# One group of eight PSUM banks for every accumulator, in a two-layer hybrid encoder

## The chip, the cores and the metric

The kernel runs on one core of one Trainium2 chip. The metric is device time in microseconds (us) of one execution, launch to end, on that core; lower is better. The profile splits the core into TensorE (PE: matmuls and transposes; PEld its weight loads), VectorE (DVE), ScalarE (ACT), GpSimd (POOL), SyncE (SP, which here only issues transfers) and the DMA engines. PE writes its results to PSUM, which has eight banks of 512 float32 per partition; a tile of this kernel's PSUM pool is one whole bank. DVE and ACT read the results from there.

## The reference, cut to what matters

Two layers, 512 tokens, width 1024, all in float32. Each layer is a feed-forward block, a mixer with three kinds of attention, and a second feed-forward block:

```
for l in range(2):
    h = h + 0.5 * rmsnorm(swiglu(rmsnorm(h), w_gu, w_down))         # FFN 1, inner width 2816
    u = rmsnorm(h); proj = u @ w_in[l]                              # q,k,v of A, B, C and the gates
    oa = neighbourhood_attention(qa, ka, va, rpb)                   # 8 heads, bias table, window on a grid
    ob = sliding_window_attention(rope(qb), rope(kb), vb, sink)     # 8 heads, |i-j| <= 128, a sink logit
    oc = differential_attention(rope(qc), rope(kc), vc, lam)        # 4 heads x 2 maps, dense 512 x 512
    merged = sum_i sigmoid(gate_i) * (o_i @ w_branch_i)
    h = h + rmsnorm(merged @ w_out)
    h = h + 0.5 * rmsnorm(swiglu(rmsnorm(h), w_gu2, w_down2))       # FFN 2
```

## The kernel before, in words

Every float32 operand is split into a high part (rounded by ACT) and a low part (the rest, by DVE), and each product of 128 x 128 blocks is three matmuls, L298, L299 and L300 in `mm3`. `dense1` (L317) makes one 128 x 512 block of a projection this way: 8 blocks deep, so 24 matmuls into one bank (12 for a branch product). The weights stream in tiles of 512 KB; ACT and DVE split them half a tile at a time (L199, L200), which serves 12 matmuls, and four such halves may wait ahead.

`bank(tag)` (L144) hands out a PSUM tile. There are three tags: `mm` with four banks (projections, FFN products), `at` with three (attention scores, transposes, small sums) and `o` with one (attention outputs and sums).

The feed-forward blocks are matmuls of the same kind (L842, L1082) with little else in between; a good part of them and the handovers stand in a region in which PE, ACT and DVE keep the order of the program text.

The mixer (L1387 on) is a list of units, `ORDER` (L68), written in this order: `qa`, `kb`, `qb`, `qc` make queries, keys and values; `aa`, `ab`, `ac` are the attention of branch A and B (one unit is two heads) and of C (one unit is one head with its two maps); `g..` are gates and `y..` the products with `w_branch`, 24 of each. Around the three kinds of attention the list reads `qa0 qa1 aa0 aa1 qa3 qa2 aa3 aa2 kb ga2 ga1 ...`, `... ab0 qb1 ...  ab1 ... ab3 ab2 ...` and `... ac0 yb0 yb1 qc2 ... ac1 ... ac2 ... ac3`. A scheduler makes from it one fixed order of instructions for each engine: it prefers what is written first and takes something written later when the first is not ready by its own reckoning or has no buffer. On the chip each engine takes its list strictly in order, except that waits are by semaphore.

One head of A or B is `softmax_pv` (L1329):

- four blocks of 128 queries: two matmuls of scores each (L1337, L1338) into an `at` bank; DVE adds the bias and takes the row extreme (L1341); ACT does the exponential and the row sum (L1350). B has two small steps for its sink (L1347 on DVE ahead of the exponentials, L1353/L1354 behind them);
- one reciprocal (L1355) and four scalings (L1357) on DVE;
- for four blocks of keys: PE transposes (L1365) into an `at` bank, ACT makes the high part (L324), DVE the low part (L325), PE multiplies both with the values into the `o` bank (L1368, L1369);
- ACT and DVE add the two halves of the `o` bank up (L1371, L1372).

The scores are ten blocks of 128 x 128 a head (2, 3, 3 and 2), so are the transposes. One head of C is `attn_c` (L1464): 16 score matmuls of 512 columns (L1475, L1476), eight row maxima (L1477) and exponentials (L1482), reciprocals, scalings and differences on DVE (L1486 to L1490), 16 transposes (L1498), 12 value matmuls (L1501 to L1503), and then a copy, a square and a row sum (L1505, L1508, L1511).

In a layer there are thus 8 heads of A, 8 of B and 4 of C.

Of the kernel before, what the change touches and what calls it, by code (L numbers as in the profile page):

```python
# [10 lines left out]
F32 = mybir.dt.float32  # L11
# [5 lines left out]
P = 128  # L17
# [3 lines left out]
T = 512  # L21
# [9 lines left out]
WARM = 9  # L31
PAD = {"f": 184, "m": 184}
SECOND = 1
KS = 8
KP = KF - 2 * KS
HOLD_OUT = ("g", "g", "g", "g", "g", "tx", "tx", "pt")
# [73 lines left out]
def encoder_kernel(ctx: ExitStack, tc: tile.TileContext, order, xT, wts, cols, rows, rpb, consts, tables, out):  # L110
# [5 lines left out]
    ps = ctx.enter_context(tc.tile_pool(name="ps", bufs=1, space=PSUM))  # L116
# [2 lines left out]

    BUFS = {"X": 6, "n": 2, "wr": 3, "wp": 4}  # L120
    ABUFS = {"f": {"t": 4, "x": 10}, "m": {"t": 5, "h": 4, "rr": 2, "tx": 5, "st": 16, "g": 10, "s": 2, "pt": 4}}
    PBUFS = {"mm": 4, "at": 3, "o": 1}

    def open_phase(kind):
        pool = ExitStack()
# [5 lines left out]
    def nm(s):  # L131
        serial[0] += 1
        return f"{s}{serial[0]}"

    def big(tag, dt=F32, shape=(P, T), name="v"):
        if tag in BUFS:
            return sb.tile(list(shape), dt, tag=tag, name=nm(name), bufs=BUFS[tag])
        kind, pool = phase[0]
        return pool.tile(list(shape), dt, tag=tag, name=nm(name), bufs=ABUFS[kind][tag])
# [2 lines left out]
        return sb.tile([P, w], F32, tag=tag, name=nm(tag), bufs=bufs)  # L142

    def bank(tag):  # L144
        return ps.tile([P, T], F32, tag=tag, name=nm(tag), bufs=PBUFS[tag])

    V, A, G, PE = nc.vector, nc.scalar, nc.gpsimd, nc.tensor

# [83 lines left out]
    def quarter(k, u):  # L232

        return KP + KS * (int(k[1]) - 1) + 2 * u, HB * (int(k[0]) - 1)

    for l in range(L):
        for which in (1, 2):
            name = f"ffn{which}_w_down"
            places = {(k, u): quarter(k, u) for k in ("11", "12", "21", "22") for u in range(KS // 2)}
            places.update({(f"n{n + 1}", u): (2 * u, HB * n) for n in range(2) for u in range(KP // 2)})  # L240
# [5 lines left out]
    def sum_up(l, which):  # L246
# [3 lines left out]
        def begin_sum(key, u):  # L250
            t = dr.tile([P, 2, T], F32, tag="sum", name=nm("sum"), bufs=L * 2 * 2 * (KS // 2))
            G.dma_start(t, down[l, which, ("21", u)])
            sums[l, which, (key, u)] = t

        def add_to(key, more, u):
            G.dma_start(sums[l, which, (key, u)], down[l, which, (more, u)], accum_op=ALU.add, max_dma_last_dim=4096)

        for key, more in (("s3", "11"), ("s1", "22")):
            steps.extend((lambda key=key, u=u: begin_sum(key, u)) for u in range(KS // 2))
            steps.extend((lambda key=key, more=more, u=u: add_to(key, more, u)) for u in range(KS // 2))  # L260
        return steps
# [14 lines left out]
    def first_loads(hT):  # L276
        def load(hs, *bs):
            for b in bs:
                nc.sync.dma_start(hT[:, b, hs], xT[b * P : (b + 1) * P, hs])

        load(HALVES[0], 0)
        fetch(2, nc.sync)
        load(HALVES[0], 1, 2)
        fetch(1, nc.sync)
        load(HALVES[0], 3, 4, 5)
        fetch(1, nc.sync)
        load(HALVES[0], 6, 7)
        load(HALVES[1], *range(KD))
        nc.sync.dma_start(cons, consts)
        warm = bank("o")  # L290
        for _ in range(WARM):
            PE.matmul(warm[:, :P], ones, ones, start=True, stop=True)
        V.tensor_scalar(out=half, in0=colt, scalar1=0.5, scalar2=None, op0=ALU.mult)
# [8 lines left out]
    def dense(blocks, X, tags=("mm",), i=None, accs=None, ws=None, midway=None, hooks={}):  # L302
        accs = accs or [bank(tags[n % len(tags)]) for n in range(len(blocks))]
        kept = []
        for k in range(len(X)):
            if midway and k == len(X) // 2:
                midway()
            x = X[k] if i is None else (X[k][0][:, i, :], X[k][1][:, i, :])
            for n, (acc, (name, l, r0, c)) in enumerate(zip(accs, blocks)):
                w = ws[k * len(blocks) + n] if ws else wblk(name, l, r0 + k, c)  # L310
                kept.append(w)
                mm3(acc if i is None else acc[:, HALVES[i]], w, x, k == 0, k == len(X) - 1)
            if k in hooks:
                hooks[k]()
        return (accs, kept) if i == 0 else accs

    def dense1(name, l, c, X, r0=0, tag="mm", midway=None):  # L317
        return dense([(name, l, r0, c)], X, (tag,), midway=midway)[0]
# [13 lines left out]
    def spread(r, nt):  # L332
        rep = bank("at")
        for t in range(nt):
            PE.matmul(
                rep[:, t * P : (t + 1) * P], r[:, t : t + 1].to_broadcast([P, P]), ident, start=True, stop=True
            )
        return rep[:, : nt * P]
# [1048 lines left out]
    def mixer(l, op, first):  # L1387
        w, X = "w_in", op.blocks
        second = [dense1(w, l, c + 1, X) for c in (QA, KA)[:SECOND]]
        cosR = big("rr", name="cosR")  # L1390
# [280 lines left out]
def build(order):  # L1671
    import concourse.bacc as bacc

    nc = bacc.Bacc("TRN2", target_bir_lowering=False, num_devices=1)
    shapes = {
        "xT": (D, T),
        "wts": (NTILES, P, WB * P),
        "cols": (P, NCOLS),
        "rows": (L * ROWW,),
        "rpb": (L * 8 * 16 * RPBW,),  # L1680
        "consts": (P, CONSTW),
        "tables": (P, TABLEW),
    }
    args = [nc.dram_tensor(f"in_{n}_dram", s, F32, kind="ExternalInput").ap() for n, s in shapes.items()]
    args.append(nc.dram_tensor("out_0_dram", (D, T), F32, kind="ExternalOutput").ap())
    with tile.TileContext(nc) as tc:
        encoder_kernel(tc, order, *args)
    return nc
# [35 lines left out]
```

## Time and profile before

| | before |
|---|---|
| time, median of 3 runs | 2442.7 us (2439.57 to 2444.72) |
| the profiled execution's own time | 2441.57 us |
| its span, first to last instruction | 2439.8 us |
| matmuls on PE | 14298 |
| busy share of PE, DVE, ACT | 99%, 74%, 55% |
| stretch from 390 to 790 us (mixer, layer 0) | 400 us, of them DVE busy 279.26 us, ACT 225.40 us |
| stretch from 1610 to 2010 us (mixer, layer 1) | 400 us, of them DVE busy 280.95 us, ACT 224.40 us |

The profile is one execution, taken by the hardware; its time is 1.1 us under the median of the runs. In its rows a group or a timeline entry names the line of the kernel, the engine, the operation, and the tiles written and read (`at<-cons,s`: writes an `at` bank, reads the constants and the scores `s`). A timeline row begins with its start in us and its length in us; in square brackets stands how long the engine was idle before and what released it. Matmuls are pipelined: the step from one start to the next is what a matmul costs, not its listed length. A windows row gives a stretch, its length, and the busy time of each engine with its number of instructions, then the clock that TensorE was granted (1.00 is full speed), the share of the DMA engines and GB/s.

### The profile page before, as it was taken

What the parts mean: (1) busy time and instruction counts of PE and PEld (TensorE: products, weight loads), DVE (VectorE), ACT (ScalarE), POOL (GpSimd) and SP (SyncE); (2) the same over time, 40 slices, a digit from 0 to 9 for tenths busy, and PEclk for the clock granted to TensorE, in tenths of its full rate; (3) what the DMA queues carried; (4) which work ended last, traced back from release to release, by engine and by line L of the source; (5) the groups of instructions that cost most, each with busy time, mean ns of one, the idle gap of its engine ahead of it and who ended that gap; (6) DMA issues with size and microseconds to landing.
All of it is one profiled execution on the core that took longest, in us unless ns stands there. A gap on an engine that the chain in (4) does not pass through costs nothing. (4 is left out here: it accounts for less than half of the span.)

```text
span 2439.8 us, 37786 instructions
## 1 busy us (share of the span) xinstructions
PE 2404.1 (99%) x14298; PEld 2111.5 (87%) x14298; DVE 1797.8 (74%) x2943; ACT 1347.5 (55%) x2471; POOL 192.1 (8%) x192
## 2 busy tenths in 40 slices
PE   9999999999999999999999999999999999999998
PEld 8999888888877889998899998888877778899987
DVE  8887976857667467888878878776676764788786
ACT  6555655646555365555655555555465554555553
POOL 0111000000111100110001110000001111011100
PEclk9999999999999999999999999999999999999999
DMA  5566536445442334654435565373454333356642
GB/s 170 162 163 182 169 132 175 116 113 149 111 131 95 111 105 132 169 154 162 170 95 157 156 173 190 116 183 106 113 143 124 110 103 121 96 147 165 184 144 87
DMA packets 119190, 340.59 MB, mean 140 GB/s; under 512 B 15968, under 2 KB 22752, under 8 KB 118496
## 3 DMA queue, kind: packets, MB, share of 16 engines
q1 hardware_dynamic: 91344, 224.85, 29.9%
q10 hardware_dynamic: 22032, 79.78, 10.9%
q0 software_dynamic: 5632, 33.56, 6.8%
q8 instruction: 112, 1.84, 0.3%
q14 instruction: 70, 0.57, 0.1%
HBM read 285.16 MB, written 48.23 MB: 137 GB/s over the span
## 5 line engine op out<-in xcount | busy, mean ns | idle before, releaser
L298 PE MATMUL mm<-X,w 128*128 128x512 f32 (+1 forms) x1044 | 397.1, 380 | 2.2 <-ACT w L199 1.7
L299 PE MATMUL mm<-X,w 128*128 128x512 f32 (+1 forms) x1044 | 396.8, 380 | 0.7 <-DVE X L522 0.7
L300 PE MATMUL mm<-X,w 128*128 128x512 f32 (+1 forms) x1044 | 396.1, 380 | 0.0
L200 DVE TENSOR_TENSOR w<-wr,w 128x512 fp32r<-128x512 f32 x360 | 255.3, 714 | 168.2 <-ACT w L199 167.0
L199 ACT ACTIVATE w<-wr 128x512 fp32r<-128x512 f32 x360 | 223.4, 627 | 226.6 <-PE mm L300 184.3
L842 PE MATMUL mm<-ht,l 128*128 128x256 f32 x1120 | 316.5, 283 | 0.0
L842 PE MATMUL mm<-ht,h 128*128 128x256 f32 x1120 | 316.3, 282 | 0.0
L842 PE MATMUL mm<-lt,h 128*128 128x256 f32 x1120 | 315.6, 282 | 0.0
L298 PEld LDWEIGHTS mm<-X,w 128*128 128x128 f32 x1044 | 197.4, 189 | 34.0 <-ACT w L199 1.9
L299 PEld LDWEIGHTS mm<-X,w 128*128 128x128 f32 x1044 | 197.2, 189 | 32.2 <-DVE X L522 1.1
L300 PEld LDWEIGHTS mm<-X,w 128*128 128x128 f32 x1044 | 197.1, 189 | 31.4
L842 PEld LDWEIGHTS mm<-ht,l 128*128 128x128 f32 x1120 | 213.1, 190 | 0.0
L842 PEld LDWEIGHTS mm<-ht,h 128*128 128x128 f32 x1120 | 213.0, 190 | 0.0
L842 PEld LDWEIGHTS mm<-lt,h 128*128 128x128 f32 x1120 | 212.7, 190 | 0.0
L1082 PE MATMUL mm<-wh,f 128*128 128x512 f32 x640 | 200.3, 391 | 0.0
L842 PE MATMUL mm<-X,h 128*128 128x256 f32 x1120 | 200.3, 279 | 0.0
L842 PEld LDWEIGHTS mm<-X,h 128*128 128x128 f32 x1120 | 171.2, 189 | 0.3
L842 PE MATMUL mm<-X,l 128*128 128x256 f32 x560 | 155.4, 278 | 0.0
L1082 PEld LDWEIGHTS mm<-wh,f 128*128 128x128 f32 x640 | 120.3, 188 | 26.9
L702 DVE TENSOR_TENSOR l<-wr,h 128x1024 fp32r<-128x1024 f32 x70 | 85.7, 1224 | 78.5 <-PE mm L842 78.5
L1082 PE MATMUL mm<-wl,f 128*128 128x512 f32 x320 | 126.6, 396 | 3.1 <-DVE wl L959 3.1
L324 ACT ACTIVATE hi<-at 128x256 fp32r<-128x256 f32 (+2 forms) x168 | 77.2, 474 | 73.4 <-PE at L1365 37.9
(366 smaller groups left out, 5458.5 us busy)
## 6 DMA issues: line engine op xcount, KB each, us to landing
wr<-in_wts_dram SPq DMA_DIRECT2D x223, 512.0 KB, 4.7
wr<-in_wts_dram ACTq DMA_DIRECT2D x152, 512.0 KB, 3.6
sum<-in_wts_dram POOLq DMA_DIRECT2D x64, 512.0 KB, 5.5
st<-hi SPq DMA_DIRECT2D x84, 128.0 KB, 2.5
st<-lo SPq DMA_DIRECT2D x84, 128.0 KB, 3.4
ap<-in_wts_dram SPq DMA_DIRECT2D x20, 512.0 KB, 6.7
a<-kept SPq DMA_DIRECT2D x32, 256.0 KB, 5.9
ap<-sum SPq DMA_DIRECT2D x16, 512.0 KB, 4.7
```

The costliest lines, as they stand in the source:

```text
L199: A.activation(hi, raw, AF.Copy)
L200: V.tensor_tensor(out=lo, in0=raw, in1=f(hi), op=ALU.subtract)
L298: PE.matmul(acc, w[0], x[0], start=start, stop=False)
L299: PE.matmul(acc, w[0], x[1], start=False, stop=False)
L300: PE.matmul(acc, w[1], x[0], start=False, stop=stop)
L324: A.activation(hi, src, AF.Copy)
L702: V.tensor_tensor(out=W[g]["l1"], in0=raws[g][0], in1=f(W[g]["h1"]), op=ALU.subtract)
L842: PE.matmul(acc, ws[i], xs[j], start=start and k == n == 0, stop=stop and k == HK - 1 and n == 2, skip_group_check=True,)
L1082: PE.matmul(acc, x[i], w[j], start=start and n == 0, stop=stop and n == 2, skip_group_check=True)
```

## The change

The dictionary of three groups goes, and all tiles of the PSUM pool get one tag with eight buffers. The names of the tiles (`mm`, `at`, `o`) stay, so the rows of both kernels can be compared.

```
+BANKS = 8
...
-    PBUFS = {"mm": 4, "at": 3, "o": 1}
...
     def bank(tag):
-        return ps.tile([P, T], F32, tag=tag, name=nm(tag), bufs=PBUFS[tag])
+        return ps.tile([P, T], F32, tag="bank", name=nm(tag), bufs=BANKS)
```

No operation is added or removed and no byte more is moved. What changes is which bank a tile gets, and with it the order that the scheduler makes. Three places of PE's order follow; a row is the line, the operation, the tile written and the tiles read, and the size; `x2` stands for two in a row.

The first is the start of unit `aa0`, the first attention of layer 0. `at_4157` to `at_4169` are the four score banks of its first head, `at_4184` to `at_4213` its transposes, `o_4183` its output bank; `mm_4461` is the first projection of unit `qa3`, which is written behind `aa0` and `aa1`. Before:

```order
L1337 MATMUL at_4157<-st_4013,st_4001 128x256
L1338 MATMUL at_4157<-sw_4016,st_4001 128x256
L1337 MATMUL at_4161<-st_4013,st_4001 128x384
L1338 MATMUL at_4161<-sw_4016,st_4001 128x384
L299 MATMUL mm_4461<-X_3643,w_4074 128x512
L300 MATMUL mm_4461<-X_3642,w_4074 128x512
L298 MATMUL mm_4461<-X_3642,w_4074 128x512
```

And now:

```order
L1337 MATMUL at_4157<-st_4013,st_4001 128x256
L1338 MATMUL at_4157<-sw_4016,st_4001 128x256
L1337 MATMUL at_4161<-st_4013,st_4001 128x384
L1338 MATMUL at_4161<-sw_4016,st_4001 128x384
L1337 MATMUL at_4165<-st_4013,st_4001 128x384
L1338 MATMUL at_4165<-sw_4016,st_4001 128x384
L1337 MATMUL at_4169<-st_4013,st_4001 128x256
L1338 MATMUL at_4169<-sw_4016,st_4001 128x256
L1365 MATMUL at_4184<-cons,s_4156 128x128 x2
L1368 MATMUL o_4183<-hi_4187,v_4032 128x256
L1365 MATMUL at_4193<-cons,s_4156 128x128 x2
L1369 MATMUL o_4183<-lo_4188,v_4032 128x256
```

Before, 53 matmuls of projections stand between the first scores of this head and its first transpose (17 behind its second pair of scores, 16 behind the third, 20 behind the fourth). Now none does: scores, transposes and value matmuls of the head follow each other.

The second is the end of the same group of units, the fourth head of `aa0` and `aa1`. `at_4447` is its last transposed bank. Before:

```order
L299 MATMUL mm_4669<-X_3645,w_4654 128x512
L300 MATMUL mm_4669<-X_3644,w_4654 128x512
L298 MATMUL mm_5059<-X_3642,w_4672 128x512
L1369 MATMUL o_4417<-lo_4422,v_4141 128x256
L1368 MATMUL o_4417<-hi_4431,v_4141 128x384
L1365 MATMUL at_4447<-cons,s_4390 128x128 x2
L299 MATMUL mm_5059<-X_3643,w_4672 128x512
```

And now:

```order
L1365 MATMUL at_4447<-cons,s_4390 128x128
L1368 MATMUL o_4417<-hi_4431,v_4141 128x384
L1365 MATMUL at_4447<-cons,s_4390 128x128
L298 MATMUL mm_4461<-X_3642,w_4074 128x512
L299 MATMUL mm_4461<-X_3643,w_4074 128x512
L1369 MATMUL o_4417<-lo_4432,v_4141 128x384
L1368 MATMUL o_4417<-hi_4441,v_4142 128x384
```

`mm_4461`, which stood within the first head before, now comes behind the last bank of the fourth. The same holds in all groups of A and B: `aa0 aa1`, `aa3 aa2`, `ab0`, `ab1` and `ab3 ab2`.

The third is unit `ac0`, the first head of C. `at_6833` to `at_6893` are its eight score banks, `at_6904` the first transposed one, `mm_6963` the first product of the unit `yb0`, written behind it. Before:

```order
L1475 MATMUL at_6851<-st_6669,st_6615 128x512
L1476 MATMUL at_6851<-sw_6672,st_6615 128x512
L298 MATMUL mm_6963<-hi_5659,w_6798 128x512
L299 MATMUL mm_6963<-lo_5660,w_6798 128x512
L300 MATMUL mm_6963<-hi_5659,w_6798 128x512
L298 MATMUL mm_6963<-hi_5938,w_6798 128x512
L299 MATMUL mm_6963<-lo_5939,w_6798 128x512
```

And now, from the last score bank on:

```order
L1475 MATMUL at_6887<-st_6669,st_6615 128x512
L1476 MATMUL at_6887<-sw_6672,st_6615 128x512
L1475 MATMUL at_6893<-st_6675,st_6618 128x512
L1476 MATMUL at_6893<-sw_6678,st_6618 128x512
L1498 MATMUL at_6904<-cons,s_6830 128x128 x4
L1501 MATMUL o_6903<-hi_6909,hi_6721 128x512
L1498 MATMUL at_6916<-cons,s_6830 128x128 x4
```

The 16 scores stand in a row, the transposes right behind them, and `mm_6963` comes behind the row sums (L1511) of the head. The other heads of C look the same.

## The prediction

> **What bounds the kernel now.** I read the share of each engine first, then the two mixer stretches by windows, then the timeline of single heads.
>
> ```profile
> PE 2404.1 (99%) x14298; PEld 2111.5 (87%) x14298; DVE 1797.8 (74%) x2943; ACT 1347.5 (55%) x2471; POOL 192.1 (8%) x192
> 390.00:790.00 400.00, 391.79 (x1927) 319.65 (x1926) 279.26 (x660) 225.40 (x500) 31.08 (x22) 1.00 0.45 123
> 1610.00:2010.00 400.00, 393.13 (x1927) 320.29 (x1926) 280.95 (x652) 224.40 (x496) 34.52 (x24) 1.00 0.43 120
> ```
>
> PE is the bound. In the span of 2439.8 us it is idle for 35.7 us in all; in the two stretches with the attention for 8.2 and 6.9, together 15.1 us, at a granted clock of 1.00. So the softmax of every head, which is a chain over DVE and ACT, is hidden behind projections on PE. Two limits follow: the change cannot win more than 35.7 us, and every us in which PE waits for a softmax is a us more.
>
> The order shows what goes: in the kernel after, PE's list has no projection inside a group of heads, and PE takes its list in order. All 16 heads of a layer in A and B and all 4 in C now expose their chains. I therefore need three numbers for each kind of head: how long its chain takes, how much of it PE works, and how many there are.
>
> **One head of A.** DVE and ACT rows of three heads of unit `aa0` and `aa1`:
>
> ```profile
> 410.45 0.41 DVE L1341 CUSTOM_DVE_ANT_0 s<-at,bedge 128x256 f32<-128x256 f32 x1
> 414.07 0.19 ACT L1350 ACTIVATION_READ_ACCUMULATOR s<-s,nmx 128x1 f32 x1
> 417.39 0.82 ACT L324 ACTIVATE hi<-at 128x256 fp32r<-128x256 f32 x2 [0.44 <-PE at L1365]
> 426.94 1.27 DVE L1357 TENSOR_SCALAR s<-s,l 128x256 f32<-128x256 f32 x4
> 428.05 0.82 ACT L324 ACTIVATE hi<-at 128x256 fp32r<-128x256 f32 x2 [1.02 <-PE at L1365]
> 431.60 0.41 DVE L1341 CUSTOM_DVE_ANT_0 s<-at,bedge 128x256 f32<-128x256 f32 x1
> 434.74 0.19 ACT L1350 ACTIVATION_READ_ACCUMULATOR s<-s,nmx 128x1 f32 x1
> 435.41 1.27 DVE L1357 TENSOR_SCALAR s<-s,l 128x256 f32<-128x256 f32 x4
> 437.32 0.77 ACT L324 ACTIVATE hi<-at 128x256 fp32r<-128x256 f32 x2 [1.87 <-PE at L1365]
> ```
>
> From the first high part of a head to the first reduction of the next: 431.60 - 428.05 = 3.55. From there to the last row sum: 414.26 - 410.45 = 3.81. To the first scaling (with the reciprocal between): 435.41 - 434.93 = 0.48. To the first high part, by way of the transposes: 428.05 - 426.94 = 1.11. Sum 8.95, taken as **9.0 us**. The bounds: 417.39 to 428.05 is 10.66 and 428.05 to 437.32 is 9.27 with projections in between; without them some delays go, and with DVE and ACT free of weight work I set the lower end half a us under the sum, at 8.5.
>
> PE's own work in such a head, from the steps between starts:
>
> ```profile
> 544.00 0.28 PE L1337 MATMUL at<-st,st 128*128 128x256 f32 x1
> 544.12 0.28 PE L1338 MATMUL at<-sw,st 128*128 128x256 f32 x1
> 544.36 0.34 PE L1337 MATMUL at<-st,st 128*128 128x384 f32 x1
> 544.53 0.34 PE L1338 MATMUL at<-sw,st 128*128 128x384 f32 x1
> 405.35 1.04 PE L1365 MATMUL at<-cons,s 128*128 128x128 f32 x8
> ```
>
> A 256 column matmul costs 0.12 and a 384 column one 0.17; eight transposes take 1.04, of which the last one's drain is no cost, so 0.11 each. Scores 4 x 0.12 + 4 x 0.175 = 1.2, value matmuls the same, ten transposes 1.1: 3.5 us. PE idles 9.0 - 3.5 = 5.5 us a head; 16 heads in two layers give **88 us** (8.5 to 10.7: 80 to 115).
>
> **One head of B.** Its exponentials wait for L1347, which waits for all four reductions:
>
> ```profile
> 545.14 0.41 DVE L1341 CUSTOM_DVE_ANT_0 s<-at,cons 128x256 f32<-128x256 f32 x1
> 547.73 0.08 DVE L1341 DVE_READ_ACCUMULATOR2_ANT nmx<- 128x1 f32 x1
> 548.93 0.23 DVE L1347 TENSOR_SCALAR nmx<-nmx,nsink 128x4 f32<-128x4 f32 x1
> 549.19 0.51 ACT L1350 ACTIVATE s<-s,nmx 128x256 f32<-128x256 f32 x1 [0.19 <-DVE nmx L1347]
> 552.12 1.28 DVE L1357 TENSOR_SCALAR s<-s,l 128x256 f32<-128x256 f32 x4
> 553.23 0.82 ACT L324 ACTIVATE hi<-at 128x256 fp32r<-128x256 f32 x2 [0.41 <-PE at L1365]
> 557.06 0.41 DVE L1341 CUSTOM_DVE_ANT_0 s<-at,cons 128x256 f32<-128x256 f32 x1
> ```
>
> High part to next reduction 557.06 - 553.23 = 3.83; reductions 547.81 - 545.14 = 2.67; L1347 directly behind (the 1.1 us here are weight work put between) 549.19 - 548.93 = 0.26; exponentials to scaling 2.93; scaling to high part 1.11. Sum 10.8. PE works 3.5, so 7.3 us idle; 16 heads give **117 us** (10 to 12: 104 to 136).
>
> **One head of C.**
>
> ```profile
> 681.27 0.39 PE L1475 MATMUL at<-st,st 128*128 128x512 f32 x1
> 681.50 0.39 PE L1476 MATMUL at<-sw,st 128*128 128x512 f32 x1
> 682.49 1.28 DVE L1477 TENSOR_REDUCE nm<-at 128x1 f32<-128x512 f32 x2
> 695.43 0.75 DVE L1490 SCALAR_TENSOR_TENSOR s<-s,lc,e 128x512 f32<-128x512 f32 x1
> 704.49 1.02 PE L1511 MATMUL at<-ones,sqt 128*128 128x1 f32 x8
> L1477 DVE TENSOR_REDUCE nm<-at 128x1 f32<-128x512 f32 x64 | 42.7, 682 | 7.3 <-PE at L1476 7.3
> L1490 DVE SCALAR_TENSOR_TENSOR s<-s,lc,e 128x512 f32<-128x512 f32 x32 | 26.4, 825 | 0.1
> L1487 DVE TENSOR_SCALAR e<-e,lc,misc 128x512 f32<-128x512 f32 x32 | 17.9, 559 | 0.1
> ```
>
> The DVE part took 13.7 us here (682.49 to 696.18), part of it waiting for scores that projections held up; its busy time is (42.7 + 26.4 + 17.9) / 8 = 10.9. With all scores issued in a row I take 11.7, nearer to the busy time. Ahead of it are two scores and their drain (0.7), behind it transposes, splits, value matmuls, copy, square: 704.49 - 696.18 = 8.3, and the row sums, 0.3. That is 21.0. PE works (16 + 12) x 0.23 + 16 x 0.11 + 0.5 = 8.7, and waits 12.3; 8 heads give **98 us** (DVE part 10.9 to 13.7: 92 to 114). PE now also waits between the last value matmul and L1511, since the projections that stood ahead of the row sums are behind them.
>
> **Sum at full clock.** 88 + 117 + 98 = 303. Projections still fill the last value matmuls of each of ten groups (0.8 each, seen in the order), and the first head of a group has no L1372 of a predecessor in its chain: -10 (0 to -15). The 15.1 us that PE idled there before are in these numbers already: -15. The feed-forward blocks keep PE's order but for their first few rows, and their matmuls hide what moves: 0 (-5 to +5, the waits that PE has there now being of some us each way). So +278, and 2441.6 + 278 = 2719.6.
>
> **The clock.** Idle stretches of this length hardly exist before. The one long one is at the very end:
>
> ```profile
> 9.00:10.00 1.00, 0.06 (x1) 0.00 (x0) 0.59 (x2) 1.00 (x3) 0.00 (x0) 1.00 1.04 396
> 1.00 4.21 PE L292 MATMUL o<-ones 128*128 128x128 f32 x18 [1.00 <-POOL eps L271]
> 6.72 0.42 PE L300 MATMUL mm<-X,w 128*128 128x256 f32 x1
> 7.34 0.28 PE L299 MATMUL mm<-X,w 128*128 128x256 f32 x1
> 2433.77 1.01 PE L512 MATMUL at<-cons,a 128*128 128x128 f32 x4 [2.85 <-DVE a L464]
> 2434.00:2435.00 1.00, 1.00 (x7) 0.88 (x6) 0.56 (x2) 0.00 (x0) 0.00 (x0) 0.50 0.03 7
> ```
>
> After 2.85 us without a matmul the granted clock is 0.50. At the start PE worked from 1.0 to 6.9 us at about half speed (the last slow matmul 0.42 long, the same kind soon after 0.28) before it was released: 5.9 us, a loss of up to 2.95. In the new kernel PE is idle from the last score to the first transpose of the next head: about 3.5 us in A, 5 in B, 8 in C. So I expect the clock to fall in all of B and C and in half of A. What that costs: of a head's 3.5 us of PE work at half clock 3.5 more, of which part lies beside DVE and ACT; bounds 0 and 3.5, taken 1.7. A 8 x 1.7, B 16 x 1.7, C half of the 5.0 us behind its reductions, 8 x 2.5, and 18 restarts of projections (9 a layer) at 2.2 (0 to 2.95): 14 + 27 + 20 + 40 = **+101** (0 to 205).
>
> [...]
>
> **Forecast.** 2441.6 + 278 + 101 = 2820.6; the profiled run lay 1.1 under the median: about **2820 us**.
>
> **Rivals.**
> - The clock holds, because bursts of 3.5 us of PE work in each head keep it up: 2720. For it: from 9 to 10 us PE worked 0.06 us and the clock stayed at 1.00. Against it: the end of the trace.
> - The clock stays at half through all attention and the chains take most of it: 32 heads x 2.5, C 8 x 3.75, restarts 18 x 2.95: 163, hence 2885.
> - Not slower: the shared banks let PE put all scores of a head down at once and start the next head early, so that PE's idle time goes instead of growing; at most 35.7 us less, 2405. It decides from the point at which a head's chain of 9 us falls to PE's own 3.5. The scalings alone take 1.28 of that, and the order still has the next head's scores behind the transposes of this one; I see little for it. [...]
>
> ```profile
> PE at L1337 <- DVE nmx L1341: 2.7, 2, 1.5
> PE at L1365 <- DVE s L1357: 1.0, 3, 0.4
> ```
>
>   That is 2.7 us in two waits, and 1.0 in three.
> - Neutral: projections are hidden elsewhere, PE's idle time stays near 36 us and the time near 2442. The order speaks against it.
>
> **How the numbers follow.** Forecast 55%, clock held 22%, half clock throughout 17%, not slower by the banks 3%, neutral or other 3%. The bounds of the chains are -30 to +50 about the sum, the clock's 0 to 205. The range 2700 to 2900 holds the forecast, nearly all of the held clock and most of half clock. A measurement here tells 0.2% (5 us) from no change: faster by more 2%, within 2%, slower 96%.
>
> **What would show it.** PE busy near 2400 to 2500 in a span near 2820; waits of PE at L1365 for L1357 and at L1498 for L1490 as the longest, some 4 us each; the first now 1.0 us in all; heads of A 9 us apart, of B 10.8, of C 21 long; a granted clock below 1 in the mixer stretches and 1.00 in the feed-forward. A mixer stretch of about 590 in place of 400 us. Wrong would be: projections between the heads on the chip, a chain that shrinks by a third without them, or a clock at 1.00 throughout.

## The result and the profile after

| | before | after |
|---|---|---|
| time, median (range), 4 runs each on the same chip | 2442.6 us (2439.57 to 2444.72) | 2919.6 us (2917.33 to 2920.88) |
| ratio, 95% interval | | 1.195 (1.193 to 1.197) |
| span of the profiled execution | 2439.8 us | 2917.8 us |

The kernel is slower by 477 us. The forecast of 2820 had the direction, but lies 100 us too low, and the time is 20 us above the range. One execution of ten of the kernel mm_apart below took 6890.1 us, with no cause known, and is left out of its ratio.

From the page of the changed kernel, busy time of the engines and the granted clock in 40 slices:

```profile
PE 2548.6 (87%) x14298; PEld 2223.1 (76%) x14298; DVE 1810.0 (62%) x2943; ACT 1363.1 (47%) x2471; POOL 191.3 (7%) x192
PEclk9999978977887899999999999789877889999999
```

The same 14298 matmuls keep PE busy 2548.6 - 2404.1 = 144.5 us longer. Nearly all of that is the lower clock: while the granted clock was 0.50, PE was busy for 281.5 us, and half of that, 141, is what full speed would have saved (an estimate). PE is idle for 2917.8 - 2548.6 = 369.2 us in place of 35.7, which is 333.5 more. The two make up the 478.0 us of span. By windows (length; busy PE, PEld, DVE, ACT, POOL; clock; DMA share; GB/s):

```profile
390.00:700.00 310.00, 226.44 (x964) 188.30 (x964) 152.74 (x387) 121.09 (x283) 6.87 (x5) 0.82 0.29 81
700.00:1000.00 300.00, 209.14 (x831) 163.66 (x832) 122.43 (x255) 102.01 (x202) 19.98 (x14) 0.81 0.27 76
1000.00:1400.00 400.00, 397.78 (x2558) 360.90 (x2558) 281.32 (x367) 209.85 (x345) 42.98 (x42) 1.00 0.45 133
```

All of it is in the mixer; the feed-forward stretch is as full as in the kernel before, where PE was busy for 397.8 of the 400 us from 800 to 1200, at a clock of 1.00. What PE waited for in the whole span, longest in total first (us in total, times, longest):

```profile
PE at L1365 <- DVE s L1357: 158.0, 32, 12.0
PE at L1318 <- ACT x L1425: 98.4, 16, 12.0
PE at L1498 <- DVE s L1490: 28.2, 16, 2.0
PE at L1498 <- DVE nm L1478: 27.8, 16, 2.3
PE o L1368 <- ACT hi L324: 17.1, 34, 0.5
PE at L1511 <- ACT sqt L1508: 11.3, 8, 1.4
PE o L1501 <- ACT hi L324: 5.7, 9, 0.7
```

The first row is the 32 heads of A and B, and the rows of L1498, L1501 and L1511 are C: both were forecast. The second was not. Before, the list of waits had for it:

```profile
PE at L1318 <- ACT x L1425: 3.0, 4, 1.5
```

L1318 transposes the values in the units `qa`, `kb` and `qc`; in the last two a rotation stands ahead of it, and they have 94 of the 98.4 us. One of its waits in the changed kernel, unit `qc`, from the timelines of PE, ACT, DVE and POOL:

```profile
738.92 0.39 PE L300 MATMUL mm<-X,w 128*128 128x512 f32 x1
749.88 1.12 PE L1318 MATMUL at<-cons,x 128*128 128x128 f32 x4 [10.57 <-ACT x L1425]
738.07 0.60 ACT L1376 ACTIVATE raw<-mm 128x512 f32<-128x512 f32 x1 [0.48 <-DVE w L200]
748.72 0.63 ACT L324 ACTIVATE hi<-x 128x512 fp32r<-128x512 f32 x1 [8.74 <-DVE x L1384]
749.25 0.58 ACT L1425 ACTIVATE x<-mm 128x512 f32<-128x512 f32 x1
747.99 0.69 DVE L1384 TENSOR_TENSOR x<-x,sh 128x512 f32<-128x512 f32 x1 [6.88 <-POOL sh L1383]
746.69 1.26 POOL L1383 TENSOR_TENSOR sh<-sh,sinR 128x512 f32<-128x512 f32 x1 [10.50 <-DMA sh<-raw]
```

PE ends the projection of the values at 739. The copy of them, L1425, stands on ACT behind the high part of the rotated keys. The rotation copies the keys out (738.07), sends them through a transfer, multiplies on POOL (746.69) and adds on DVE (747.99): some 10 us. Before, later projections ran on PE meanwhile. Now the bank of the transposes is of the projections' group, and none of them can be put ahead of it.

Four heads of A, first transposes of each, on PE:

```profile
403.95 0.71 PE L1365 MATMUL at<-cons,s 128*128 128x128 f32 x2 [11.98 <-DVE s L1357]
413.91 0.71 PE L1365 MATMUL at<-cons,s 128*128 128x128 f32 x2 [3.07 <-DVE s L1357]
424.56 0.71 PE L1365 MATMUL at<-cons,s 128*128 128x128 f32 x2 [3.77 <-DVE s L1357]
434.51 0.71 PE L1365 MATMUL at<-cons,s 128*128 128x128 f32 x2 [3.07 <-DVE s L1357]
```

They come 10.0, 10.7 and 10.0 us apart, not 9.0; the waits inside are 3 to 4 us, not 5.5, since PE's own work takes longer at the low clock: by windows from one of these rows to the next PE is busy 6.4 us a head, not 3.5, at a granted clock of 0.66 to 0.67 (0.64 from 400 to 436 us).

### The profile page after: what moved, and what is told of

Same layout as the page of the kernel before. It is cut to its first block, busy times and chain, and to the rows that moved or that the text cites. A ratio compares the mean times of both kernels' runs of the same rounds, so it can differ in the third digit from the quotient of the medians.

```text
span 2917.8 us, 37857 instructions
## 1 busy us (share of the span) xinstructions
PE 2548.6 (87%) x14298; PEld 2223.1 (76%) x14298; DVE 1810.0 (62%) x2943; ACT 1363.1 (47%) x2471; POOL 191.3 (7%) x192
## 5 line engine op out<-in xcount | busy, mean ns | idle before, releaser
L200 DVE TENSOR_TENSOR w<-wr,w 128x512 fp32r<-128x512 f32 x360 | 247.0, 691 | 316.9 <-ACT w L199 316.2
L298 PE MATMUL mm<-X,w 128*128 128x512 f32 (+1 forms) x1044 | 406.7, 390 | 2.7 <-ACT w L199 2.0
L299 PE MATMUL mm<-X,w 128*128 128x512 f32 (+1 forms) x1044 | 402.0, 385 | 0.7 <-DVE X L522 0.7
L300 PE MATMUL mm<-X,w 128*128 128x512 f32 (+1 forms) x1044 | 400.0, 383 | 0.0
L298 PEld LDWEIGHTS mm<-X,w 128*128 128x128 f32 x1044 | 205.0, 196 | 39.9 <-ACT w L199 2.2
L1365 PE MATMUL at<-cons,s 128*128 128x128 f32 x320 | 95.0, 417 | 158.0 <-DVE s L1357 158.0
L299 PEld LDWEIGHTS mm<-X,w 128*128 128x128 f32 x1044 | 203.8, 195 | 37.2 <-DVE X L522 1.1
L300 PEld LDWEIGHTS mm<-X,w 128*128 128x128 f32 x1044 | 202.9, 194 | 37.2
L1365 PEld LDWEIGHTS at<-cons,s 128*128 128x128 f32 x320 | 60.5, 199 | 168.7 <-issue 137.2
L325 DVE TENSOR_TENSOR lo<-at,hi 128x256 fp32r<-128x256 f32 (+2 forms) x168 | 90.1, 538 | 127.1 <-ACT hi L324 118.2
```

Of the source, the lines that this page charges most:

```text
L200: V.tensor_tensor(out=lo, in0=raw, in1=f(hi), op=ALU.subtract)
L298: PE.matmul(acc, w[0], x[0], start=start, stop=False)
L299: PE.matmul(acc, w[0], x[1], start=False, stop=False)
L300: PE.matmul(acc, w[1], x[0], start=False, stop=stop)
L325: V.tensor_tensor(out=lo, in0=src, in1=f(hi), op=ALU.subtract)
L1365: PE.transpose(tp[:, (i - i0) * P : (i - i0 + 1) * P], ss[i][:, c : c + P], ident)
```

## The experiments

One run each unless said; the kernel before, beside them, took 2439.8 to 2444.9 us (medians).

**Which groups.** Three kernels differ from the changed one in the two lines that make the groups (the new lines, in this order mm_apart, mm_with_o and mm_with_at; the last line is the same in all):

```
+GROUP, BANKS = {"mm": "mm", "at": "at", "o": "at"}, {"mm": 4, "at": 4}
+GROUP, BANKS = {"mm": "mm", "at": "at", "o": "mm"}, {"mm": 5, "at": 3}
+GROUP, BANKS = {"mm": "mm", "at": "mm", "o": "o"}, {"mm": 7, "o": 1}
+        return ps.tile([P, T], F32, tag=GROUP[tag], name=nm(tag), bufs=BANKS[GROUP[tag]])
```

> Two groups of four: projections (mm) have four banks of their own, attention tiles and outputs (at, o) share the other four. Theory (order): a projection cannot be put ahead of a waiting attention unit once both draw on one group, because tiles of one group are handed out in the order of the text; with mm apart it can again. In the order, 786 projection matmuls stand between the last scores and the first transposes of the 40 heads here, 788 in the kernel before, none in the changed kernel. So about 2440 us, within 10 of before, PE idle below 45 us. Rival (capacity): heads lose because transposes, scores and outputs compete for too few banks of a mixed group; then this kernel, whose attention has four mixed banks, is clearly slower than before, 2500 us or more.

Measured over three rounds: 2446.9 us, ratio to before 1.0023 (1.0013 to 1.0033). The eight banks in two groups, with the projections apart, lose 6 us, not 477, as the theory has it; the rival's 2500 is out. The longest wait in its list of PE's waits:

```profile
PE at L1365 <- DVE s L1357: 6.4, 3, 2.4
```

> Five banks for projections and attention outputs together (mm, o), three for at. Theory (order): the output bank of a head is handed out behind its softmax, and now no later projection can pass it; the order has no projection between scores and transposes in any head. So near the changed kernel: 2850 to 2950 us, PE at L1365 waiting for L1357 some 160 us in 32 waits. The wait of the V transposes (L1318 for L1425, 98 us after the change) goes down, since their bank comes from at, which is apart: below 20 us, if projections may pass it. Rival (capacity): at is as before and mm has one bank more, so near before, 2440 to 2500 us.

Measured: 2793.4 us, below the expected band but far from the rival. The scores' group is as it was before, and only the output bank stands among the projections: +352 us. The longest of PE's waits, and one of C's at L1498:

```profile
PE at L1365 <- DVE s L1357: 131.0, 32, 7.8
PE at L1318 <- ACT x L1425: 23.4, 12, 3.9
PE at L1475 <- ACT s L1482: 17.0, 14, 2.3
PE at L1337 <- DVE nmx L1341: 14.0, 5, 7.1
PE at L1498 <- DVE s L1490: 9.6, 19, 0.8
```

The heads of A and B wait 32 times, as foretold, but 131 us in place of some 160. The V transposes, whose bank is apart here, wait 23.4 us, a little over the 20 expected and far under 98.4; C's transposes wait less than I had in mind. The two rows of L1475 and L1337, 31 us, are scores that wait for one of the three banks of their own group.

> Seven banks for projections and at together, one for the outputs (o) as before. Theory (order): again no projection between scores and transposes in any head, so 2900 to 2960 us, with both waits of the changed kernel, 158 us at L1365 and 98 us at L1318. Rival (the single mixed group with the output bank in it is what costs): clearly under 2850 us.

Measured: 2872.3 us, with 158.8 us at L1365 and 98.4 at L1318. The waits are as expected; the time is 28 us below the band and above the rival's 2850. The 47 us under the changed kernel are the output bank's, to which o_late returns. mm_with_o and mm_with_at give the projections' group more banks than before, and both are slow: what decides is which tiles share a group with the projections.

**Which unit.** Four kernels start from before and put the banks of one kind of unit into the projections' group of four; all else stays. The edit for A (for B the two words are the other way round, C has three such places) and for the V transposes:

```
-    def bank(tag):
-        return ps.tile([P, T], F32, tag=tag, name=nm(tag), bufs=PBUFS[tag])
+    def bank(tag, group=None):
+        return ps.tile([P, T], F32, tag=group or tag, name=nm(tag), bufs=PBUFS[group or tag])
...
-            sp = bank("at")[:, :n]
+            sp = bank("at", "at" if sink else "mm")[:, :n]
...
-            tp = bank("at")[:, :n]
+            tp = bank("at", "at" if sink else "mm")[:, :n]
```

```
     def turn(x, heads):
-        tp = bank("at")
+        tp = bank("at", "mm")
```

> The kernel before (groups of four, three and one; 2441 us) with one thing changed: the score and transposed banks of the A heads come out of the projections' group. In the order no projection stands inside the 16 A heads then; B, C and the V transposes are as before. By the prediction's terms: 88 for the chains, 14 for the clock in the heads, 4 restarts of 2.2, some 5 less at the group ends, so +106 and about 2547 us. By the trace of the changed kernel, in which these heads wait 70 us at L1365 and PE works at half speed in parts of them: the same size, 2525 to 2555. Rival (the parts are not additive; most of the loss is one shared wait): under 2480 us.

> The same for the B heads alone. By the prediction's terms: 117 for the chains, 27 for the clock in the heads, 6 restarts of 2.2, some 5 less at the ends, so +152 and about 2593 us. By the trace of the changed kernel (88 us of waits at L1365 in these heads, 12.0 us from head to head in place of 10.8): 2570 to 2600. Rival: under 2520 us.

> The same for the C heads alone (all their at tiles from the group of four). By the prediction's terms: 98 for the chains, 20 for the clock, 8 restarts of 2.2, so +136 and about 2577 us. By the trace of the changed kernel, where C waits 73 us in all at L1498, L1501 and L1511: about 2540 to 2560. Rival: under 2500 us.

> The same for the bank of the V transposes (L1318) alone: ten units, kb and the four qc in each layer and the qa units. The prediction has no term for it: 2441 us by its sum. Theory now: the unit's projections cannot be followed by later ones, so PE waits for the rotation ahead of L1425, 98.4 us in the changed kernel, and restarts ten times at 2.2: +120, about 2560 us if it is additive; at least the 68 to 73 us that v_first and turn_in_o took back, so 2510 to 2565. Rival: 2450 us or less, the wait being one that only arises together with the attention in the same group.

Measured, against 2443.6 us of before beside them, with the busy time of PE from each page (only_a, only_b, only_c, only_turn, in this order):

```profile
PE 2437.7 (96%) x14298; PEld 2139.8 (84%) x14298; DVE 1806.7 (71%) x2943; ACT 1352.4 (53%) x2471; POOL 192.2 (8%) x192
```

```profile
PE 2447.4 (95%) x14298; PEld 2143.3 (83%) x14298; DVE 1811.6 (70%) x2943; ACT 1349.2 (52%) x2471; POOL 190.3 (7%) x192
```

```profile
PE 2474.8 (96%) x14298; PEld 2148.9 (84%) x14298; DVE 1793.2 (70%) x2943; ACT 1351.7 (53%) x2471; POOL 192.1 (7%) x192
```

```profile
PE 2428.2 (97%) x14298; PEld 2125.9 (85%) x14298; DVE 1797.1 (72%) x2943; ACT 1350.4 (54%) x2471; POOL 189.8 (8%) x192
```

| | time | more than before | PE busy more than 2404.1 | PE idle more than 35.7 | by the prediction |
|---|---|---|---|---|---|
| only_a | 2540.4 | 97 | 34 | 65 | 106 |
| only_b | 2576.0 | 132 | 43 | 91 | 152 |
| only_c | 2568.7 | 125 | 71 | 57 | 136 |
| only_turn | 2506.4 | 63 | 24 | 41 | 0 |

(Idle is the span, 2538.6, 2574.2, 2567.0 and 2504.7 us, less the busy time.) All four rivals fall. The parts of A, B and C are each 8 to 13% smaller than forecast, and the fourth, for which the forecast has no term, is worth 63 us, just under the band of 2510 to 2565. Together they are 417 us. These kernels also put more tiles into a group of four, which the changed kernel, with eight, does not: in only_c scores (L1475) wait 12.3 and 6.8 us for an exponential to leave a bank. And in only_turn L1318 itself waits only 15.6 us; the longest row is C's scores waiting 18.7 us for a bank of their three (L1475 for L1482). So each figure is the price of that one change of group, not the length of one wait.

**The V transposes in the changed kernel.** Two ways to take that wait away. v_first moves code only:

```
-            sq = stacks(rope(dense1(w, l, QC + hd, X), cosR, sinR), False)
+            v = dense1(w, l, VC + hd, X)
+            q = dense1(w, l, QC + hd, X)
+            vt = turn(plain(v, False), 1)
+            sq = stacks(rope(q, cosR, sinR), False)
             sk = stacks(rope(dense1(w, l, KC + hd, X), cosR, sinR), True)
-            return sq, sk, turn(plain(dense1(w, l, VC + hd, X), False), 1)
+            return sq, sk, vt
```

(and likewise in `kb`). turn_in_o is mm_with_at with one bank drawn elsewhere:

```
     def turn(x, heads):
-        tp = bank("at")
+        tp = bank("o")
```

> The changed kernel with one thing moved: in the units kb and qc the values are projected first and turned (L1318) before the rotation of queries and keys, so that the copy L1425 no longer stands on ACT behind the high part of the rotated keys. Theory (the part that the prediction left out): the 98.4 us that PE waits at L1318 go nearly all, and with them about ten restarts at half clock of some 2 us each; 2919.6 - 98 - 20 = about 2800 us (2785 to 2825), waits at L1365 unchanged at 158. Rival: the rotation only moves its wait to the scores of the next attention unit, L1475 and L1337; then 2890 us or more with the new waits there.

> The kernel mm_with_at (seven banks for mm and at, one for o; 2872.3 us) with the bank of the V transposes (L1318) taken from the o group, nothing else moved. Theory: L1318 waits 98.4 us only because the transposes' bank is of the projections' group and later projections may not pass it; apart from it they can, so the wait falls below 15 us and with it the restarts: 2872 - 98 - 10 = about 2764 us (2750 to 2800; the upper end if, as in v_first, some 20 us come back as waits of scores for the stacks' transfers). Rival: what L1318 waits for is late whatever the group; then 2860 us or more.

Measured: 2851.3 us, 68 less than the changed kernel, and 2799.2, 73 less than mm_with_at. The wait goes, but not all of it is won: v_first misses its band of 2785 to 2825, and turn_in_o ends at the upper edge of its own, with 17.8 us left at L1318. Some of PE's waits in v_first:

```profile
PE at L1318 <- ACT x L1425: 15.4, 8, 5.9
PE at L1475 <- DMA st<-lo: 9.2, 4, 4.3
PE at L1476 <- DMA sw<-hi: 7.1, 2, 3.6
```

Of 98.4 us 83 are gone, and 16 come back as waits of C's scores for the transfers of the rotated queries and keys: a part of the rival. The rows of L1498 grow as well, from 56.0 to 64.8 us. The price of this unit in the changed kernel is 68 to 73 us.

**The output bank.** o_late is the changed kernel with the output bank taken later and the value matmuls written one block later; in A and B (C likewise; lines in between are left out at `...`):

```
-        op = bank("o")
+        ready = []
...
+            ready.append((j, i0, i1, *split(tp, "pt", shape=(P, n))))
+            if j == 1:
+                op = bank("o")
+            while ready and j and (len(ready) > 1 or j == NT - 1):
+                k, i0, i1, hi, lo = ready.pop(0)
+                o = op[:, i0 * P : i1 * P]
+                PE.matmul(o, vof(k), hi, start=k == 0, stop=False, skip_group_check=True)
+                PE.matmul(o, vof(k), lo, start=False, stop=k == NT - 1, skip_group_check=True)
```

> The changed kernel with the output bank of each head taken behind the second block of transposes (and its value matmuls written one block later), in A, B and C. Nothing else moves. Theory: with the output bank in the same group, the first value matmul must go ahead of the second block's transposes, so PE waits for the high part in every head (17.1 us at L1368, 5.7 at L1501, and late transposes in C); mm_with_at, which has the output bank apart, is 47 us faster. Written later it should give the same: 2919.6 - 47 = about 2872 us (2860 to 2890), the waits for the high part under 4 us. Rival (the 47 us came from the number of banks left for the rest, seven against eight with a different rotation): 2905 us or more.

Measured: 2874.8 us, 45 less; mm_with_at had given 47. The row of the value matmuls (now L1372) that stood at 17.1 us:

```profile
PE o L1372 <- ACT hi L324: 0.4, 2, 0.2
```

In one group, the output bank, written ahead of the loop over the keys, goes ahead of the second transposed bank, so that the first value matmul waits for ACT in each head with nothing to do. The two rows of the value matmuls, 17.1 and 5.7 us, come down to 0.4 and 3.8; the rest of the 45 us is spread over the other waits and PE's busy time (2531.6 us). The rival falls: the number of banks is the same in both.

**The clock.** warm adds matmuls that only work and whose result nothing reads, between scores and transposes:

```
+    def fill(n, q, k):
+        wm = bank("o")
+        for _ in range(n):
+            PE.matmul(wm, q, k, start=True, stop=True)
...
+        fill(22 if sink is None else 30, qs, sk[0])
...
+            fill(26, qs, sk[0][0])
```

> The changed kernel with extra matmuls that nothing reads, put between the scores and the first transposes of every head: 22 of 512 columns in A, 30 in B, 26 in C (5.0, 6.8 and 5.9 us at full clock, into a bank that is taken and released there). They add work to PE in its waits and nothing else. Theory (clock on the path): the lower granted clock is caused by PE's waits and stretches every head; with PE at work the clock holds in the heads, A heads come 9.0 apart in place of 10.0 and B heads 10.8 in place of 12.0, so although PE has 236 us more to do the time falls to about 2840 us (2815 to 2865); the restarts behind the V transposes stay. Rival (the clock costs nothing on the path): the heads keep their 10 and 12 us and the time is 2919 or more.

> v_first (2851.3 us) with the same extra matmuls. Theory: the two effects are apart, so again about 80 us less: 2770 us (2745 to 2800), granted clock above 0.97. This is the state in which only the softmax chains are exposed, at full clock; the prediction priced it at 2720. Rival: no gain, 2851 or more.

> warm with fewer extra matmuls, since in warm the extra ones of A and B ended 0.9 to 1.7 us behind the scaling that the transposes wait for: 14 in A, 22 in B, 26 in C as there. Theory: what the clock costs within the heads is the prediction's 14 + 27 + 20 = 61 us: 2919.6 - 61 = about 2858 us (2840 to 2875), heads of A 9.2 or less and of B 11.0 or less apart. If the shorter fill lets the clock fall again, the granted clock in the stretch from 400 to 450 us is below 0.9 and the time stays near 2900. Rival (the clock costs nothing in the heads): 2905 us or more at a clock of 0.95 or more.

Measured: warm 2900.1 and v_first_warm 2833.3, each some 19 us less than without, not 80, so both miss their bands: the extra matmuls of A and B were longer than the waits that they filled. warm2, with 14 and 22 in place of 22 and 30, took 2859.0 us, as expected: 61 us less than the changed kernel, though PE has 784 matmuls more to do. Its first transposes in heads of A, then of B:

```profile
414.12 0.57 PE L1366 MATMUL at<-cons,s 128*128 128x128 f32 x2
422.87 0.57 PE L1366 MATMUL at<-cons,s 128*128 128x128 f32 x2 [0.58 <-DVE s L1358]
431.37 0.57 PE L1366 MATMUL at<-cons,s 128*128 128x128 f32 x2 [0.26 <-DVE s L1358]
618.15 0.66 PE L1366 MATMUL at<-cons,s 128*128 128x128 f32 x2 [0.28 <-DVE s L1358]
628.19 0.57 PE L1366 MATMUL at<-cons,s 128*128 128x128 f32 x2
```

With PE at work two heads of A come 8.8 and 8.5 us apart and two of B 10.0. Two transposes take 0.57 to 0.66 us in these rows, 0.71 in the four of the changed kernel; the granted clock was 0.90 from 400 to 450 us and 1.00 from 590 to 610, where the changed kernel has 0.70 and 0.60. Within the groups of heads of layer 0 the steps are 8.0 to 8.8 us in A, save the first pair at 10.2, where the changed kernel has 9.4 to 10.7; in B they are 10.0 to 10.4, where it has 11.9 to 12.6. A head of C takes 21.4 to 22.7 us from its first score to its row sums in both kernels: there the extra matmuls hold the first transposes back by some 3.5 us.

**Only the order.** gaps keeps one group of eight and writes units of projections into the heads, between scores and transposes (with the values first, as in v_first); gaps2 places them better, puts one ahead of the row sums of C and takes the output bank late. Of the list of units, in gaps2, behind each `:` what is written into the first and the second head:

```
+qa0 qa1 ga0 aa0:ga1:ga2 aa1:ga3:ga4 qa3 qa2 aa3:ga5:ga6 aa2:ga7:kb qb0 qb1 ya5 ya0
+ab0:qb3:qb2,ya1 ab1:ya2,ya3,ya4:ya6,ya7 ab3:gb4:gb0 ab2:qc0:qc1 gb1
+ac0:yb0,gb2:yb1 qc2 ac1:yb2,gb3:yb4 qc3 gb5 ac2:yb5,gb6:yb3
...
+            def gap(s):
+                for v in inner[s].split(",") if inner else ():
+                    do(v)
...
+        gap()
         if sink is not None:
```

> One group of eight banks as in the changed kernel, values first as in v_first, and the units of projections written by hand inside the heads: between the scores and the transposes of a head stand now one to three units of 12 or 24 matmuls (gates in A; y units, queries and keys in B; y units and gates in C), 1128 matmuls in all 40 heads. Theory (only the order of handing out matters, not how many banks or groups there are): PE has work in the chains again, the waits at L1365 fall below 30 us, the clock holds and the time comes to within 2% of before, 2440 to 2490 us. Rival (sharing one group costs in itself, by waits for banks): 2600 us or more, with waits of PE for a bank's readers.

> gaps with the places mended where it still waited: a gate unit ahead of the first head, kb and the queries of B earlier, more projections in the heads of B and C (1344 matmuls in 40 heads), one ahead of the row sums of C, and the output bank late as in o_late. Still one group of eight. Theory (only the order of handing out matters): 2470 to 2540 us, PE idle under 110 us. Rival (one group costs in itself): no better than 2600 us.

Measured: 2643.4 and 2558.2 us. Both miss their bands. By its time gaps lies in the rival's range, 2600 us or more, but not by its waits: the longest are 41.4 us for scaled scores, 25.6 for a transfer and 21.4 for the high part, not for a bank's readers. 276 and 361 of the 477 us come back with the single group kept. Of these 68 are the values first, as v_first has them alone, and in gaps2 some 45 the late output bank, by o_late; against v_first, the units inside the heads are worth 2851.3 - 2643.4 = 208 us in gaps. What gaps2 still waits for, the first five rows:

```profile
PE at L1504 <- DVE s L1495: 25.8, 24, 2.2
PE at L1337 <- DMA st<-hi: 21.6, 2, 10.9
PE o L1373 <- ACT hi L324: 14.7, 30, 2.0
PE at L1366 <- DVE s L1358: 14.2, 7, 2.9
PE at L1480 <- ACT s L1487: 5.1, 2, 2.8
```

The first four are results that PE needs; of these five only the last, a score that waits for an exponential to leave its bank, is a wait for a bank. PE idles for 116.0 us, a little above the 110 expected. I take the rest of the loss to be what my order by hand did not cover; that a perfect order would reach 2442 with one group was not shown.

## Why the prediction was right, and where it failed

- **Mechanism and sign: right.** No projection passes a waiting unit of its own group, PE stands (idle for 369.2 us in place of 35.7), and the clock falls (0.922 on average over the span in place of 0.999). mm_apart (+6 us) shows it, and the gaps kernels support it from the other side. The rivals "not slower" and "neutral" are out: all eight banks were handed out in both kernels, PE's wait for scores to leave a bank was 2.7 us in all before (L1337 for L1341), and the one group is 19.5% slower.
- **The step that failed** is "All 16 heads of a layer in A and B and all 4 in C now expose their chains. I therefore need three numbers for each kind of head". The list was not complete, since it went by softmax, while the rule holds for every tile of the group. Two more take banks of it: the V transposes of `kb` and `qc`, with the rotation ahead of them (68 to 73 us), and the output bank ahead of the second transposed bank (45 to 47 us). Together 113 to 120 us, more than the 100 us by which the forecast was low; the terms of the heads, which were too large, take some of it back.
- **The terms of the heads** were a little too large. A, with its clock and restarts, 106 against 97; B 152 against 132; C 136 against 125. For A and B a part of the reason is in the chains: 9.0 and 10.8 were taken, mostly 8.0 to 8.8 and 10.0 to 10.4 are there in warm2. In C the parts differ more than the sum: less idle time (57 us, not 98) and more PE time (71 us). The granted clock of only_c was 0.973 on average over 2567.0 us, that of the kernel before 0.999 over 2439.8: 69 and 2 us at full speed were not granted, so that at most some 67 of the 71 are the clock (an estimate), where the forecast had 20 and restarts of 18.
- **The clock in the heads**, 14 + 27 + 20 = 61 us: warm2 won 61, but that the sums agree is luck. By the steps between heads in layer 0, warm2 wins 1.3 us for a head of A and 2.1 for one of B, about 20 and 33 us for the 16 of each (an estimate), and next to nothing in C, where the extra matmuls take the place of the waits. A and B were thus set too low, and C's term is not shown. That the clock would fall in only half of the heads of A, the 8 of 8 x 1.7, was the author's estimate, which no run shows: in layer 0 it fell in all 8. The 40 us for restarts were not measured alone.
- **The sum as the runs have it:** 97 + 132 + 125 for the heads, 68 to 73 and 45 to 47 for the two that were missed, 467 to 474 of 477 us. With the 63 us of only_turn it is 462 to 464. So 3 to 15 us have no owner; the parts were measured in different surroundings and need not add up.
- **The rivals on the clock.** "The clock holds" (2720) is out. "Half clock throughout" (2885; its own terms give 2883) is nearer to the time, but for the wrong reason: the granted clock was 0.81 to 0.82 in the mixer, and between the heads of A, where it was 0.64 from 400 to 436 us, it came back to 1.00 each time.
- **The signs foretold:** the wait at L1365 is the longest, 158.0 / 32 = 4.9 us each, against some 4; those at L1498 are 1.8 us each and not 4, because C's transposes wait four times for one row block each. (The row of L1498 that names L1478 is the same wait: in the first head of C L1490 ends at 805.54 and L1478, next on DVE, at 805.66, and PE goes on at 805.68.) The steps between heads are 9.4 to 10.7 us in A, not 9, and 11.7 to 13.4 in B, not 10.8; a head of C takes 21.4 to 22.7 us to its row sums, near the 21. The clock is below 1 in the mixer and 1.00 in the feed-forward, as foretold. PE is busy 2548.6 us, above the 2500 that I gave. The mixer grew by some 477 / 2 = 239 us a layer, not by 190.

## What to carry to other kernels

When buffers are merged into one group, go through every place of the program that takes one from it, not only the waits that you have in mind: in this program each that waits held back what is written behind it and needs the same group. Two groups, one for the work that fills and one for the work that waits, cost 6 us here, one group 477; the best order by hand with one group was still 113 us slower than before (2558.2 against 2444.9). And the total of a wait in the list is not its price: 98.4 us at L1318 were worth 68 to 73 when they were taken away.

## What the runs showed of the hardware

I had expected the clock to fall after stretches in which PE does nothing. In the changed kernel it also fell after stretches in which PE worked for part of the time, in the first row below for 1.29 us of 3.41. Windows of 3.41 us in the heads of A in the changed kernel (length; busy PE, PEld, DVE, ACT, POOL; clock):

```profile
409.55:412.96 3.41, 1.29 (x9) 1.08 (x7) 3.26 (x12) 2.68 (x8) 0.00 (x0) 1.00 0.01 3
412.96:416.38 3.42, 1.94 (x8) 1.59 (x8) 2.66 (x9) 0.58 (x3) 0.00 (x0) 0.50 0.23 77
416.38:419.79 3.41, 3.41 (x14) 3.33 (x14) 1.76 (x4) 1.36 (x3) 0.00 (x0) 0.50 0.01 2
419.79:423.20 3.41, 1.00 (x7) 0.79 (x6) 2.75 (x10) 2.79 (x9) 0.00 (x0) 1.00 0.00 0
423.20:426.62 3.42, 1.53 (x6) 1.19 (x6) 3.23 (x10) 0.88 (x4) 0.00 (x0) 0.50 0.23 77
```

In this trace the clock is 1.00 or 0.50 and nothing between. All its stretches but the first and the last are whole multiples of 3.4133 us to within 0.001: at 0.50 they are 3.41 us (10 of them), 6.83 (23), 10.24 (20) and 13.65 (4) long, at 1.00 the longest is 839.68 us, from 1003.47 to 1843.15. Of 171 windows of 3.4133 us in a row from 409.55, one at 1.00 was followed by one at 0.50 in 26 cases, in 7 of which PE had done nothing and in 10 of which it had been busy for 1.00 to 2.00 us; it stayed at 1.00 after 85, with at least 1.59 us busy. From 0.50 it rose after 25 windows with 2.85 us or more, and stayed after 34 with 2.95 or less. The mixer of layer 1 (185 windows from 1843.15) gives much the same: it fell with up to 2.38 us, held with at least 1.60, stayed low with up to 2.92 and rose with at least 3.21. So in both mixers no window at 1.00 with more than 2.38 us of work was followed by a fall, and none at 0.50 with less than 2.85 by a rise. The clock fell once in every head of A of layer 0, 8 times in 8 heads (at 395.90, 412.96, 423.20, 433.44, 481.23, 491.47, 498.30 and 508.54 us), not in every second one as the prediction took.
